# Later tokens' scores in one stretch over four banks, and norm sums as two split products with ones

## The chip, the core and the metric

The kernel runs on one core of a Trainium2 chip, in one launch. A core has TensorE (matrix products from SBUF into the eight banks of PSUM; PE in the trace, PEld its weight loads), VectorE (DVE), ScalarE (ACT) and GpSimd (POOL), each with a queue of its own that it works off in order, and SyncE (SP), which here issues the transfers from and to memory. The metric is device time in microseconds of one execution; less is better.

## The reference, cut to what matters

Two layers work on 256 tokens of a prompt and 32 later tokens of another request, 288 columns in all, with a model width of 1024. A layer is

```
x += 0.5 * swiglu1(rmsnorm(x))                      # 1024 -> 2816 -> 1024
z  = rmsnorm(x) @ w_in                              # 1024 -> 2560: q, k, v | pool | conv
x += concat(diffattn(q, k, v), pool(u), conv(...)) @ w_out
x += 0.5 * swiglu2(rmsnorm(x))
rmsnorm(x) = x / sqrt(mean(x*x) + 1e-6) * gain
```

The attention has 4 heads, each with two halves of 64 channels. Each half has scores and a softmax of its own, and the head's weights are `softmax(half 0) - lam * softmax(half 1)`. A later token attends to 512 cached keys and to the 32 new ones. The final norm follows the second layer. Everything is float32, and the result has to agree to nearly that accuracy.

## The kernel before, in words

Tokens lie along the free dimension: x is eight tiles of [128 channels, 288 tokens]. A weight product in full precision is made of three products in the format float32r, which runs at the ordinary pace of the array: a number is split into a high part and a remainder, and `mm3` (L247) issues high x high, remainder x high and high x remainder. Weights arrive in chunks of 1 MB; ScalarE copies a chunk to its high part `wh` (L108; in the mixer through L477), and VectorE subtracts to get the remainder `wl` (L109; L477). The same is done to x (`xh`, `xl`) behind each residual. Plain float32 products are left where both operands are activations: scores, turnings, weighted sums, the pooling's small product, and sums over channels by a product with ones.

The norm is put off: the products run on x times gain, and the result is multiplied by R, one over the root of the mean square of a token. The sum of squares over the eight tiles is one tile `ssum` [128, 288]; its sum over the 128 partitions comes from TensorE. There are three ways. `stats_a` and `stats_last` (first and last norm, not changed) and the mixer's `stats` (L514) take three products of one column with `ssum` as weights, so that tokens lie on partitions, raise to the power -0.5 on GpSimd, put the three columns on diagonals, and spread them by a float32 product of ones with the diagonals (L528); sinR and cosR read that product's bank, then ScalarE copies it to R. `stats_wide` (L228, the three later FFNs) multiplies ones by `ssum` in float32 (L231), so that each partition has the sums, and VectorE gets 1/sqrt by a bit trick and three Newton steps.

TensorE's instructions run in the order of the code. In `ffn` the code of `stats_wide` stands after the fifth of eight k tiles of the first pair of products (L319), and the other engines' instructions are ordered by the tile framework: by the age of an instruction in the code, among those that are ready. In `mixer` the order of ScalarE, VectorE and GpSimd is written out by hand too, by a planner. All work beside the projections is a task in stages. A clock counts 0.369 us per triple of products, costs of the other engines are added up per queue (`charge`), and a stage is issued once its operands should stand by that clock (`poll`). A stage that needs a PSUM buffer asks for it with `wait("sc")` (one buffer of two banks, for scores) or `wait("tp")` (two buffers of one bank, for all that is turned or summed); each request adds LAG 0.2 and MARGIN 1.1 us to its time.

`attn_s` (L664) is the later tokens' attention. For each half it asks for the score buffer, makes the scores of the four heads over 544 keys in two blocks of 272, head h in output partitions 32h to 32h+31 (L673), takes the maximum over both blocks, and makes the exponentials with their sum. The halves follow each other through the one buffer. Then come the combination, five turnings, the product with the values (L708) and `finish`, which splits the result into operands of the output projection. That projection takes its input tiles in the order 4, 5, 0, 1, 2, 3, 6, 7, two at a time; the later tokens' result is asked for with tile 0 (L864). Before the mixer's products a dummy activation loads ScalarE's table for exponentials (L832), behind the first half of the output projection one loads the table for SiLU (L871).

Of the kernel before, what the change touches and what calls it, by code (L numbers as in the profile page):

```python
# [9 lines left out]
F32 = mybir.dt.float32  # L10
# [8 lines left out]
P = 128  # L19
# [37 lines left out]
def tile_step(ctx, tc, xT, w_gu, w_dn, w_in, w_out, par, con, lamv, ck, cvp, pw,  # L57
# [66 lines left out]
    ones = const.tile([P, P], F32, tag="ones", name="ones")  # L124
    V.memset(ones, 1.0)
    act0 = const.tile([P, 1], F32, tag="act0", name="act0")
# [17 lines left out]
    def warm_up(n):  # L144
        """keeps the tensor engine's clock up while it has to wait"""
        warm = ps_a.tile([P, 512], F32, tag="acc", name="warm")
        for _ in range(n):
            PE.matmul(warm[:, 0:P], ones, ones, start=True, stop=True)
# [3 lines left out]
    make_identity(nc, ident)  # L152
    mhalf = const.tile([P, 3], F32, tag="mhalf", name="mhalf")
    G.memset(mhalf, -0.5)

# [5 lines left out]
    def operands(k, g):  # L161
        """x tile k is final for this phase: operands of the next products"""
# [6 lines left out]
    def square(k, apart=0):  # L169
        """sum of squares"""  # L170
# [17 lines left out]
    def stats_a():  # L188
        """1/rms per token, tokens on partitions, then on the diagonals of [128, T]"""
# [7 lines left out]
    def stats_last(part, pss):  # L197
        """the same at the end: the sum over the tiles before the last one goes ahead"""
# [28 lines left out]

    def stats_wide():  # L228
        """1/rms per token on all partitions at once: bit trick and three Newton steps"""
        ps = ps_t.tile([P, 512], F32, tag="tp", name="ps_w")  # L230
        PE.matmul(ps[:, :T], ones, ssum[0], start=True, stop=True)  # L231
# [25 lines left out]
    # lambda of each layer, the gains of the head norm  # L257
# [91 lines left out]
    def mixer(l, g_next):  # L349
        with tc.tile_pool(name="mp", bufs=1) as mp, tc.tile_pool(name="mt", bufs=2) as mt, \  # L350
# [18 lines left out]
            # Everything beside the projections' products is a task in stages. A stage is issued once its  # L369
            # operands should stand, by a clock of the products issued so far and of the other engines'  # L370
            # queues, so that no queue is held up for long by what it waits for.
# [82 lines left out]
            def wait(res=None, cost=0.0, dep=None):  # L454
                return (0.0, res, cost, dep)
# [58 lines left out]
            def stats():  # L514
                ps = ps_t.tile([P, 512], F32, tag="tp", name="ps_ss")
                for b, (t0, _, _) in enumerate(TB):
                    PE.matmul(ps[:, b:b + 1], ssum[0][:, t0:t0 + P], ones[:, 0:1], start=True, stop=True)
                a = tmp.tile([P, 3], F32, tag="rs_a", name="rs_a")
                V.tensor_scalar(a, ps[:, 0:3], 1.0 / D, EPS, ALU.mult, ALU.add)
                r = tmp.tile([P, 3], F32, tag="rs_r", name="rs_r")  # L520
                G.tensor_tensor(r, a, mhalf, ALU.pow)
                yield wait()
                dg = tmp.tile([P, T], F32, tag="rs_d", name="rs_d", bufs=1)
                for b, (_, o, n) in enumerate(TB):
                    V.tensor_scalar(dg[:, b * P:b * P + n], ident[:, o:o + n], r[:, b:b + 1], None, ALU.mult)
                yield wait()
                ps = ps_t.tile([P, 512], F32, tag="tp", name="ps_r")
                PE.matmul(ps[:, :T], ones, dg, start=True, stop=True)  # L528
                V.tensor_tensor(sinR, con_t[:, K_SIN:K_SIN + T], ps[:, :T], ALU.mult)
                V.tensor_tensor(cosR, con_t[:, K_COS:K_COS + T], ps[:, :T], ALU.mult)  # L530
                yield wait()
                R[0] = tmp.tile([P, T], F32, tag="R", name="R")
                S.activation(R[0], ps[:, :T], AF.Copy)
# [97 lines left out]
            def finish(o, s1, n, dst, key):  # L631
                """o: PSUM [q, n blocks of e]; normalise over e, turn, scale, split into the mix operands"""
# [31 lines left out]
            def attn_s():  # L664
                yield wait(dep=("q", 3))
                yield wait(dep=("k", 3))
                for c in range(2):
                    yield wait("sc", 1.0)
                    sc = ps_s.tile([P, 2, 512], F32, tag="sc", name="scs")
                    r = slice(64 * c, 64 * c + 64)  # L670
                    for b in range(2):
                        for h in range(H):
                            PE.matmul(sc[32 * h:32 * h + 32, b, 0:272], qT[h][r, SEQ:T],  # L673
                                      kts[r, h, b * 272:(b + 1) * 272], start=True, stop=True)
                    yield wait()
                    nm = mt.tile([P, 1], F32, tag="nms", name="nms")
                    V.tensor_reduce(nm, sc[:, :, 0:272], AX.XY, ALU.max)
                    V.tensor_scalar(nm, nm, -0.125, None, ALU.mult)
                    yield wait()
                    S.activation(es_t[:, c, :].rearrange("p (b k) -> p b k", b=2), sc[:, :, 0:272], AF.Exp,  # L680
                                 scale=0.125, bias=nm, accum_out=sms[:, c:c + 1])
                    release("sc")
                yield wait()
                fr = mt.tile([P, 1], F32, tag="frs", name="frs")
# [320 lines left out]
```

## Time and profile before

| what | value |
|---|---|
| median of 3 runs | 1085.14 us (1084.9, 1085.14, 1089.98) |
| profiled execution, span from first to last instruction | 1083.4 us (the page gives no other time of this execution) |
| TensorE busy | 1070.1 us (99%), 8100 matmuls |
| VectorE busy | 702.3 us (65%) |
| ScalarE busy | 529.7 us (49%) |
| GpSimd busy | 50.0 us (5%) |
| granted TensorE clock, mean | 0.997 |

The stages, in us from the start of the span: first norm and start to 25.9, first FFN to 223.6, mixer to 331.8, second FFN to 542.4; layer 1 the same way: to 752.9, 861.2, 1072.0; then the last norm. TensorE's busy time overlaps from one matmul to the next, and the ends of matmuls are modelled; so a product's cost is read from the starts of the matmuls around it. A float32 call shows as two instructions, x2.

### The profile page before, as it was taken

What the parts mean: (1) busy time and instruction counts of PE and PEld (TensorE: products, weight loads), DVE (VectorE), ACT (ScalarE), POOL (GpSimd) and SP (SyncE); (2) the same over time, 40 slices, a digit from 0 to 9 for tenths busy, and PEclk for the clock granted to TensorE, in tenths of its full rate; (3) what the DMA queues carried; (4) which work ended last, traced back from release to release, by engine and by line L of the source; (5) the groups of instructions that cost most, each with busy time, mean ns of one, the idle gap of its engine ahead of it and who ended that gap; (6) DMA issues with size and microseconds to landing.
All of it is one profiled execution on the core that took longest, in us unless ns stands there. A gap on an engine that the chain in (4) does not pass through costs nothing.

```text
span 1083.4 us, 19614 instructions
## 1 busy us (share of the span) xinstructions
PE 1070.1 (99%) x8100; PEld 1058.2 (98%) x8100; DVE 702.3 (65%) x1191; ACT 529.7 (49%) x920; POOL 50.0 (5%) x78
## 2 busy tenths in 40 slices
PE   8999999999999999999999999999999999999997
PEld 7999999999999999999999999999999999999997
DVE  7766664547878766654576666554779786666442
ACT  6444444448755444444444444443785644444431
POOL 6000000011200000000000000000112000000000
PEclk9999999999999999999999999999999999999999
DMA  7544444445445444444444444444444354444421
GB/s 277 200 175 156 160 185 162 156 166 170 139 157 194 177 174 155 160 172 175 156 156 174 178 155 160 173 173 164 169 140 155 124 230 171 180 156 158 174 97 44
DMA packets 33897, 178.66 MB, mean 165 GB/s; under 512 B 7808, under 2 KB 10624, under 8 KB 13328
## 3 DMA queue, kind: packets, MB, share of 16 engines
q1 hardware_dynamic: 33456, 176.90, 45.5%
q8 instruction: 63, 1.03, 0.4%
q10 hardware_dynamic: 288, 0.44, 0.1%
q14 instruction: 26, 0.21, 0.1%
q0 software_dynamic: 64, 0.07, 0.0%
HBM read 173.80 MB, written 3.61 MB: 164 GB/s over the span
## 4 chain that ended last, share of the span: by engine, by line
PE 70%; issue 23%; ACT 3%; DVE 2%; DMA 1%; SPq 0%; POOLq 0%; POOL 0%; DVEq 0%; ACTq 0%
PE acc L250 22%; PE acc L251 22%; PE acc L252 22%; ACT zw L477 2%; ACT e L477 1%; ACT wh L477 1%; PE sc L250 1%; PE sc L251 1%; DMA xall<-in_xT 1%; PE sc L252 1%; DVE wl L477 0%; PE scs L673 0%; PE sc L587 0%; DVE wl L109 0%; DVE yg L899 0%
## 5 line engine op out<-in xcount | busy, mean ns | idle before, releaser
L250 PE MATMUL acc<-xh,wh 128*128 128x288 f32 x1664 | 495.9, 298 | 0.0
L251 PE MATMUL acc<-xh,wl 128*128 128x288 f32 x1664 | 493.0, 296 | 1.3 <-DVE wl L477 0.6
L252 PE MATMUL acc<-xl,wh 128*128 128x288 f32 x1664 | 491.1, 295 | 2.7 <-DVE xl L167 2.7
L109 DVE TENSOR_TENSOR wl<-raw,wh 128x1024 fp32r<-128x1024 f32 (+2 forms) x272 | 328.5, 1210 | 189.8 <-ACT wh L108 189.6
L108 ACT ACTIVATE wh<-raw 128x1024 fp32r<-128x1024 f32 (+2 forms) x272 | 280.4, 1034 | 301.8 <-PE acc L252 261.9
L252 PEld LDWEIGHTS acc<-xl,wh 128*128 128x128 f32 x1664 | 314.8, 189 | 3.6 <-DVE xl L167 3.6
L250 PEld LDWEIGHTS acc<-xh,wh 128*128 128x128 f32 x1664 | 314.7, 189 | 2.3 <-issue 1.3
L251 PEld LDWEIGHTS acc<-xh,wl 128*128 128x128 f32 x1664 | 313.0, 188 | 3.5 <-DVE wl L477 1.8
L250 PE MATMUL acc<-hh,wh 128*128 128x288 f32 x704 | 208.4, 296 | 0.0
L251 PE MATMUL acc<-hh,wl 128*128 128x288 f32 x704 | 207.7, 295 | 0.0
L252 PE MATMUL acc<-hl,wh 128*128 128x288 f32 x704 | 207.0, 294 | 0.0
L252 PEld LDWEIGHTS acc<-hl,wh 128*128 128x128 f32 x704 | 132.6, 188 | 0.0
L251 PEld LDWEIGHTS acc<-hh,wl 128*128 128x128 f32 x704 | 132.2, 188 | 0.0
L250 PEld LDWEIGHTS acc<-hh,wh 128*128 128x128 f32 x704 | 131.9, 187 | 0.0
L297 ACT ACTIVATE hh<-t 128x288 fp32r<-128x288 f32 x88 | 38.9, 444 | 107.9 <-DVE t L296 107.9
L477 DVE TENSOR_TENSOR wl<-raw,wh 128x512 fp32r<-128x512 f32 x112 | 76.6, 700 | 5.9 <-ACT wh L477 5.8
L477 ACT ACTIVATE wh<-raw 128x512 fp32r<-128x512 f32 x112 | 65.6, 627 | 6.6 <-PE acc L252 4.1
L298 DVE TENSOR_TENSOR hl<-t,hh 128x288 fp32r<-128x288 f32 x88 | 40.1, 457 | 40.0 <-ACT hh L297 39.8
L291 DVE TENSOR_TENSOR t<-acc,R 128x288 f32<-128x288 f32 x84 | 38.3, 456 | 32.4 <-PE acc L252 32.3
L294 ACT ACTIVATE t<-t 128x288 f32<-128x288 f32 x88 | 37.5, 426 | 7.6 <-DVE t L291 7.6
L296 DVE TENSOR_TENSOR t<-t,t 128x288 f32<-128x288 f32 x88 | 39.5, 450 | 0.0
L342 DVE SCALAR_TENSOR_TENSOR xall<-acc,xall 128x288 f32<-128x288 f32 x32 | 14.6, 456 | 37.0 <-PE acc L252 36.8
(181 smaller groups left out, 773.6 us busy)
## 6 DMA issues: line engine op xcount, KB each, us to landing
raw<-in_w_gu SPq DMA_DIRECT2D x86, 1024.0 KB, 4.8
raw<-in_w_dn SPq DMA_DIRECT2D x44, 1024.0 KB, 4.8
raw<-in_w_in SPq DMA_DIRECT2D x20, 1024.0 KB, 4.8
raw<-in_w_out SPq DMA_DIRECT2D x8, 1024.0 KB, 5.0
kts<-in_ck SPq DMA_DIRECT2D x2, 1024.0 KB, 5.4
cvt<-in_cv SPq DMA_DIRECT2D x2, 1024.0 KB, 7.2
raw<-in_w_gu SPq DMA_DIRECT2D x2, 512.0 KB, 7.4
out<-k SPq DMA_DIRECT2D x8, 128.0 KB, 1.7
```

What stands on the lines that cost most here:

```text
L108: S.activation(wh[:, sl, :], src, AF.Copy)
L109: V.tensor_tensor(wl[:, sl, :], src, wh[:, sl, :].bitcast(F32), ALU.subtract)
L250: PE.matmul(acc, wh[:, b, :], mh, start=first, stop=False)
L251: PE.matmul(acc, wl[:, b, :], mh, start=False, stop=False)
L252: PE.matmul(acc, wh[:, b, :], ml, start=False, stop=last)
L291: V.tensor_tensor(t1, ag[:, :T], R, ALU.mult)
L294: S.activation(t1, t1, AF.Silu)
L296: V.tensor_tensor(h, t1, t2, ALU.mult)
L297: S.activation(hh[j], h, AF.Copy)
L298: V.tensor_tensor(hl[j], h, hh[j].bitcast(F32), ALU.subtract)
L342: V.scalar_tensor_tensor(xs[m], acc[:, :T], 0.5, xs[m], ALU.mult, ALU.add)
L477: return f(out, *a, **kw)
```

## The change

Later tokens' scores: `attn_s` asks for the score buffer and for both "tp" buffers, and then makes all scores in one stretch: first 32 columns (the new keys) of each head and half into the two "tp" banks, then 512 columns (the cached keys) into the two banks of the score buffer, half c in a bank of its own. The 32 columns are copied to SBUF and the "tp" buffers given back, four small reductions and a maximum give the two halves' maxima, and the exponentials are made in four pieces whose sums are added.

Norm sums: `spread_split` splits `ssum` into a float32r high part (ScalarE) and a remainder (VectorE), and `spread_sum` multiplies both by ones in float32r. `stats_wide` takes its sums from there, and the mixer's `stats` too, which then has the sums on all partitions: ScalarE takes the root, VectorE the reciprocal and one Newton step, and sinR, cosR and R come from SBUF. The dummy activation ahead of the mixer now loads the table for the root, and one behind the root loads that for exponentials. Comments that were taken out are left out here.

```
+    ones_r = const.tile([P, P], F32R, tag="ones_r", name="ones_r")
...
+    V.tensor_copy(ones_r, ones)
...
+    eps_t = const.tile([P, 1], F32, tag="eps", name="eps")
+    G.memset(eps_t, EPS)
...
+    def spread_split(S, V):
+        sh = tmp.tile([P, T], F32R, tag="rs_u", name="rs_h", bufs=1)
+        sl = tmp.tile([P, T], F32R, tag="rs_y", name="rs_l", bufs=1)
+        S.activation(sh, ssum[0], AF.Copy)
+        V.tensor_tensor(sl, ssum[0], sh.bitcast(F32), ALU.subtract)
+        return [sh, sl]
+    def spread_sum(parts):
+        ps = ps_t.tile([P, 512], F32, tag="tp", name="ps_w")
+        for n in range(2):
+            PE.matmul(ps[:, :T], ones_r, parts[n], start=n == 0, stop=n == 1)
+        parts.clear()
+        return ps
     def stats_wide():
-        ps = ps_t.tile([P, 512], F32, tag="tp", name="ps_w")
-        PE.matmul(ps[:, :T], ones, ssum[0], start=True, stop=True)
+        ps = spread_sum(spread_split(S, V))
...
             def stats():
-                ps = ps_t.tile([P, 512], F32, tag="tp", name="ps_ss")
-                for b, (t0, _, _) in enumerate(TB):
-                    PE.matmul(ps[:, b:b + 1], ssum[0][:, t0:t0 + P], ones[:, 0:1], start=True, stop=True)
-                a = tmp.tile([P, 3], F32, tag="rs_a", name="rs_a")
-                V.tensor_scalar(a, ps[:, 0:3], 1.0 / D, EPS, ALU.mult, ALU.add)
-                r = tmp.tile([P, 3], F32, tag="rs_r", name="rs_r")
-                G.tensor_tensor(r, a, mhalf, ALU.pow)
-                yield wait()
-                dg = tmp.tile([P, T], F32, tag="rs_d", name="rs_d", bufs=1)
-                for b, (_, o, n) in enumerate(TB):
-                    V.tensor_scalar(dg[:, b * P:b * P + n], ident[:, o:o + n], r[:, b:b + 1], None, ALU.mult)
-                yield wait()
-                ps = ps_t.tile([P, 512], F32, tag="tp", name="ps_r")
-                PE.matmul(ps[:, :T], ones, dg, start=True, stop=True)
-                V.tensor_tensor(sinR, con_t[:, K_SIN:K_SIN + T], ps[:, :T], ALU.mult)
-                V.tensor_tensor(cosR, con_t[:, K_COS:K_COS + T], ps[:, :T], ALU.mult)
-                yield wait()
-                R[0] = tmp.tile([P, T], F32, tag="R", name="R")
-                S.activation(R[0], ps[:, :T], AF.Copy)
+                parts = spread_split(S, V)
+                yield wait()
+                ps = spread_sum(parts)
+                r = tmp.tile([P, T], F32, tag="R", name="R")
+                a = tmp.tile([P, T], F32, tag="rs_d", name="rs_w", bufs=1)
+                u = tmp.tile([P, T], F32, tag="rs_y", name="rs_t", bufs=1)
+                S.activation(r, ps[:, :T], AF.Sqrt, scale=1.0 / D, bias=eps_t)
+                nc.scalar.activation(act0, r[:, 0:1], AF.Exp, scale=0.0)
+                charge("act", 1.4)
+                V.tensor_scalar(a, ps[:, :T], 1.0 / D, EPS, ALU.mult, ALU.add)
+                yield wait()
+                V.reciprocal(r, r)
+                V.tensor_tensor(u, r, r, ALU.mult)
+                V.scalar_tensor_tensor(u, u, -0.5, a, ALU.mult, ALU.mult)
+                V.scalar_tensor_tensor(r, u, 1.5, r, ALU.add, ALU.mult)
+                R[0] = r
+                yield wait()
+                V.tensor_tensor(sinR, con_t[:, K_SIN:K_SIN + T], r, ALU.mult)
+                V.tensor_tensor(cosR, con_t[:, K_COS:K_COS + T], r, ALU.mult)
...
             def attn_s():
                 yield wait(dep=("q", 3))
                 yield wait(dep=("k", 3))
+                yield wait("sc")
+                yield wait("tp")
+                yield wait("tp", 1.3)
+                tn = [ps_t.tile([P, 512], F32, tag="tp", name="scn") for _ in range(2)]
+                sc = ps_s.tile([P, 2, 512], F32, tag="sc", name="scs")
+                for dst, k0, n in ((tn, PAST, DEC), ([sc[:, 0, :], sc[:, 1, :]], 0, PAST)):
+                    for h in range(H):
+                        for c in range(2):
+                            r = slice(64 * c, 64 * c + 64)
+                            PE.matmul(dst[c][32 * h:32 * h + 32, 0:n], qT[h][r, SEQ:T], kts[r, h, k0:k0 + n],
+                                      start=True, stop=True)
+                yield wait()
+                sn = mt.tile([P, 2, DEC], F32, tag="sn", name="sn", bufs=1)
                 for c in range(2):
-                    yield wait("sc", 1.0)
-                    sc = ps_s.tile([P, 2, 512], F32, tag="sc", name="scs")
-                    r = slice(64 * c, 64 * c + 64)
-                    for b in range(2):
-                        for h in range(H):
-                            PE.matmul(sc[32 * h:32 * h + 32, b, 0:272], qT[h][r, SEQ:T],
-                                      kts[r, h, b * 272:(b + 1) * 272], start=True, stop=True)
-                    yield wait()
-                    nm = mt.tile([P, 1], F32, tag="nms", name="nms")
-                    V.tensor_reduce(nm, sc[:, :, 0:272], AX.XY, ALU.max)
-                    V.tensor_scalar(nm, nm, -0.125, None, ALU.mult)
-                    yield wait()
-                    S.activation(es_t[:, c, :].rearrange("p (b k) -> p b k", b=2), sc[:, :, 0:272], AF.Exp,
-                                 scale=0.125, bias=nm, accum_out=sms[:, c:c + 1])
-                    release("sc")
-                yield wait()
+                    S.activation(sn[:, c, :], tn[c][:, 0:DEC], AF.Copy)
+                    release("tp")
+                nm = mt.tile([P, 4], F32, tag="nms", name="nms")
+                V.tensor_reduce(nm[:, 0:2], sc, AX.X, ALU.max)
+                V.tensor_reduce(nm[:, 2:4], sn, AX.X, ALU.max)
+                V.tensor_tensor(nm[:, 0:2], nm[:, 0:2], nm[:, 2:4], ALU.max)
+                V.tensor_scalar(nm[:, 0:2], nm[:, 0:2], -0.125, None, ALU.mult)
+                yield wait()
+                for c in range(2):
+                    S.activation(es_t[:, c, 0:PAST], sc[:, c, :], AF.Exp, scale=0.125, bias=nm[:, c:c + 1],
+                                 accum_out=sms[:, c:c + 1])
+                release("sc")
+                for c in range(2):
+                    S.activation(es_t[:, c, PAST:], sn[:, c, :], AF.Exp, scale=0.125, bias=nm[:, c:c + 1],
+                                 accum_out=sms[:, 2 + c:3 + c])
+                yield wait()
+                V.tensor_tensor(sms[:, 0:2], sms[:, 0:2], sms[:, 2:4], ALU.add)
...
-            nc.scalar.activation(act0, xl[0][:, 0:1].bitcast(F32), AF.Exp, scale=0.0)
+            nc.scalar.activation(act0, xl[0][:, 0:1].bitcast(F32), AF.Sqrt, scale=0.0)
```

## Rows read from the trace of the kernel before

**Rows 1.** Windows: us; busy us and instructions of PE, PEld, DVE, ACT, POOL; clock; DMA.
```profile
153.30:223.60 70.30, 70.30 (x530) 70.30 (x528) 35.74 (x46) 31.29 (x42) 0.00 (x0) 1.00 0.45 165
223.60:306.30 82.70, 81.58 (x658) 77.09 (x657) 62.69 (x163) 56.44 (x159) 15.23 (x26) 1.00 0.46 156
```

**Rows 2.** Waits of PE over the span: us in total, times, longest.
```profile
PE sc L587 <- ACT e L477: 1.4, 2, 0.7
...
PE acc L251 <- DVE wl L477: 0.6, 2, 0.3
```

**Rows 3.** Timeline (start, duration, instruction): first score stretch of later tokens.
```profile
281.70 0.29 PE L252 MATMUL acc<-xl,wh 128*128 128x288 f32 x1
...
283.22 0.29 PE L251 MATMUL acc<-xh,wl 128*128 128x288 f32 x1
```

**Rows 4.** Instructions of tile scs: count, shortest/median/longest ns.
```profile
L673 PE MATMUL scs<-kts,q x64: 389/389/413, 281.9 to 816.8; 64*32 64x272 f32 x64
L477 DVE TENSOR_REDUCE nms<-scs x4: 712/714/717, 283.9 to 818.5; 128x1 f32<-128x544 f32 x4
```

**Rows 5.** Timeline: norm sum of layer 0's second FFN.
```profile
335.95 0.65 PE L231 MATMUL ps_w<-sq,ones 128*128 128x288 f32 x2
...
336.56 0.29 PE L251 MATMUL acc<-xh,wl 128*128 128x288 f32 x1
```

**Rows 6.** Timeline, PE: scores of the first tokens, head 3.
```profile
276.81 0.29 PE L252 MATMUL acc<-xl,wh 128*128 128x288 f32 x1
277.04 0.71 PE L587 MATMUL sc<-k,q 64*128 64x256 f32 x4
277.57 0.39 PE L588 MATMUL sc<-k,q 64*128 64x128 f32 x4
...
278.14 0.29 PE L251 MATMUL acc<-xh,wl 128*128 128x288 f32 x1
```

**Rows 7.** Timeline: the mixer's norm products, layer 0.
```profile
227.73 0.72 PE L517 MATMUL ps_ss<-ones,sq 128*128 128x1 f32 x6
...
228.53 0.29 PE L251 MATMUL acc<-xh,wl 128*128 128x288 f32 x1
...
230.78 0.65 PE L528 MATMUL ps_r<-rs_d,ones 128*128 128x288 f32 x2
...
231.40 0.29 PE L251 MATMUL acc<-xh,wl 128*128 128x288 f32 x1
```

**Rows 8.** Timeline: later tokens' result, and the output projection's first product.
```profile
306.17 0.35 DVE L477 SCALAR_TENSOR_TENSOR ml<-tpo,gsub,mh 128x128 fp32r<-128x128 f32 x1
...
306.36 0.29 PE L250 MATMUL acc<-mh,wh 128*128 128x288 f32 x1
```

**Rows 9.** Timeline: the norm's end in the mixer, layer 0.
```profile
231.47 0.45 DVE L477 TENSOR_TENSOR sinR<-con,ps_r 128x288 f32<-128x288 f32 x1 [0.61 <-PE ps_r L528]
...
232.32 0.41 ACT L477 ACTIVATE R<-ps_r 128x288 f32<-128x288 f32 x1 [7.02 <-DVE cosR L477]
```

**Rows 10.** Groups by line and form, ACT: busy us, mean ns | idle before.
```profile
L832 ACT ACT_TABLE_LOAD x2 | 2.6, 1283 | 0.0
```

**Rows 11.** Timeline, DVE: around the norm sum of layer 0's second FFN.
```profile
334.69 0.45 DVE L477 TENSOR_TENSOR sq<-sq 128x288 f32<-128x288 f32 x1
...
335.66 1.22 DVE L109 TENSOR_TENSOR wl<-raw,wh 128x1024 fp32r<-128x1024 f32 x1
336.80 0.45 DVE L233 TENSOR_SCALAR rs_w<-ps_w 128x288 f32<-128x288 f32 x1
```

**Rows 12.** Timeline, DVE, ACT and PE: the same place of layer 1's first FFN.
```profile
545.40 0.45 DVE L176 TENSOR_TENSOR sq<-sq 128x288 f32<-128x288 f32 x1
...
545.94 1.06 ACT L108 ACTIVATE wh<-raw 128x1024 fp32r<-128x1024 f32 x1 [1.39 <-PE acc L252]
...
546.48 0.65 PE L231 MATMUL ps_w<-sq,ones 128*128 128x288 f32 x2
...
547.04 1.23 DVE L109 TENSOR_TENSOR wl<-raw,wh 128x1024 fp32r<-128x1024 f32 x1 [1.19 <-ACT wh L108]
```

## The prediction, on record before the changed kernel ran

> **What bounds the kernel now.** I read the windows by stage first. In a stretch of plain products TensorE is busy for the whole of it: 530 matmuls in 70.30 us, 0.133 us each, at full granted clock, while VectorE and ScalarE work about half of the time [rows 1]. The mixer's first 82.7 us hold the small work as well: TensorE is busy for 81.58, VectorE for 62.69, ScalarE for 56.44. So the sum of what TensorE issues sets the time, and a change pays only by what it takes out of TensorE's queue or by a wait that it removes there. The waits come second: outside the start TensorE waits for the scores' buffer (1.4 us in all) and for split weights (0.6 us), both in the mixers, and hardly anywhere else [rows 2]. Third the timeline, for what each small product costs TensorE beyond the pace of 0.133.
>
> **Scores of the later tokens.** Now: a stretch of 8 calls x 272 columns (16 instructions, as each float32 call is issued in two parts). The last ordinary matmul before it starts at 281.70, so the next was due at 281.83; the second one behind it starts at 283.22, so the first was due to start at 283.09. The stretch costs 1.25 us [rows 3]. There are 64 such instructions, hence four stretches, 5.0 us [rows 4].
>
> What float32 columns cost comes from the norm sum: 288 columns push the matmuls behind them from 335.95 to 336.56 less one pace, 0.48 us, or 1.66 ns a column [rows 5]. 8 x 272 columns one after the other would be 3.6 us. In 1.25 us they can only have run four heads at a time, each in its own 32 output partitions: 544 columns, 0.90 us, and 0.35 us of edges. That the two halves (operand partitions 0 to 63 and 64 to 127, two banks) overlap too is seen at the first tokens' scores: 768 columns in four calls would be 1.27 us in a row, yet they take 278.14 - 0.133 - 276.94 = 1.06 us with edges [rows 6], so 0.35 us of edges leave 0.7, about half of 1.27.
>
> After: per layer one stretch. Each of the eight places (four heads x two halves) gets 32 + 512 columns, 544, again 0.90 us if all eight run together. Edges 0.35. The 16 instructions of 32 columns: nothing below, and above 0.11 us each if they run singly, as the six one-column instructions of the old norm sum do (0.67 us / 6) [rows 7], 1.8 us. The nearest row is the present stretch, whose 16 instructions show no cost beyond columns and edges, so I take 0.15. That is 1.4 us against 2.5: 1.1 us saved a layer, **2.2 us** in all. Ends: 1.25 us saved a layer with no extra; 0.5 us lost (0.90 + 0.35 + 1.8 against 2.5).
>
> Around it: the stage now asks for the score buffer and both "tp" buffers, and the planner adds 0.2 + 1.1 us to each request, so it starts 2.6 us after the old first stretch, or behind the turning of head 3 if that takes a buffer first, near the old second one. One reduction over 1024 columns in place of 544 (0.71 us) [rows 4] adds 0.6 us, and the exponentials, now in four pieces behind it, I take at 0.9 more. The result was ready at 306.52, its first use is due 8 triples of 0.4 us after 306.36, at 309.6 [rows 8]: the 3 us of slack hide it. Without that cover 1.5 us a layer would show. Holding both "tp" buffers keeps head 3's and the pooling's small products back, which are due only behind the same point.
>
> **Norm sums in the mixers.** Removed: three one-column products, from 227.73 until 228.53 less a pace, 0.67 us, and the product that spreads the result, from 230.78 until 231.40 less a pace, 0.49 us [rows 7]. Added: two products of 288 columns in the ordinary format, two paces, 0.27 us. Saved 0.89 us a layer, **1.8 us**. Their operands need one ScalarE copy and one VectorE subtraction after the sum of squares; ScalarE stands idle for 7 us there, until 232.32 [rows 9], so they stand two microseconds before TensorE comes to them. GpSimd's power step and the diagonal go. ScalarE gets a root and a second table load (1.28 us) [rows 10]: with the two products some three triples behind 227.7, at 228.9, 0.3 for them, 0.45 for the root, 1.28 and 0.2 for the load and its dummy, it is free at 231.1, and the rotary copies that now follow the copy of R at 232.73 can start earlier. VectorE gets a reciprocal and three passes more (about 0.45 us each by the 288-column sinR row [rows 9], some 2 us), so sinR and cosR come up to 1.5 us later. Net effect on the 2.0 us of waits in the mixers: zero taken, ends -1.4 and +1.5 us a layer. No row shows a wide reciprocal; at several times a plain pass the upper end would apply.
>
> **Norm sums of the three later FFNs.** The product: 0.48 becomes 0.27, 0.21 us each, 0.6 us in all. But the place in TensorE's queue stays (after the fifth triple pair), and the copy and the subtraction are now ahead of it. In layer 0's second FFN the sum of squares starts its last addition at 334.69 for 0.45 us, done 335.14; TensorE comes at 335.95 [rows 5, 11]. The slack is 0.8 us, and ScalarE (0.41, as the copy of R) [rows 9] plus VectorE (0.45) plus hand-overs need about 1.0 if both queues are free. VectorE's isn't: at 335.66 it takes a weight remainder of 1.22 us, which was written before the norm in the code and so goes first, and only then, at 336.80, the norm's own step. The subtraction would take that place: 336.80 to 337.25, TensorE resumes about 337.3. Stall 1.35 us, and all that is queued behind on TensorE is the next FFN's products. Lower end 0.25 us (subtraction first), upper end 2.6 us (two remainders first). The same order holds in layer 1. In layer 1's first FFN the addition ends at 545.85, VectorE is then free until 547.04, and ScalarE takes a weight piece at 545.94; TensorE was due at 546.48 [rows 12]. If the copy goes ahead of that piece (it is older in the code), the stall is 0.45 us; behind it, 2.2. I take 0.45. Stalls: 2 x 1.35 + 0.45 = **3.2 us**, ends 1.0 and 7.4.
>
> **Sum.** -2.2 - 1.8 - 0.6 + 3.2 = -1.4 us on the profiled span of 1083.4, so 1082.0. The median of the runs, 1085.14, lies 1.74 us above that span (the page gives no time of its own for the profiled run); 1082.0 + 1.7 = **1083.7 us**.
>
> The Trainium skill, "TensorE: Matmul & The Clock Gate", Part 3, states that matmuls start and end strictly in program order. The code writes 256 and 128 columns of one half and then of the other, and the trace has all four 256-column instructions ahead of the four 128-column ones [rows 6]: what reaches the engine is not the code's order, so the halves of one call need not follow each other. If the new stretch did reach it as written, that rule gives the first rival below.
>
> **Rivals.**
> (1) The halves don't pair with the heads: only neighbouring calls overlap, the two halves of a head, and the heads follow each other: 4 x 0.90 + 0.35 = 3.95 us a layer against 2.5. It speaks for it that the new loop has the halves innermost; against it that [rows 6] show instructions regrouped across calls. Then +2.9 in place of -2.2: 1088.8 us, slower than before; it decides once a stretch takes over 2.1 us, where the total passes 1085.1.
> (2) The FFN stalls stay small, because the copy and the subtraction are put ahead of the weight work: 3 x 0.3 in place of 3.2 gives 1081.4; with ScalarE's earlier start taking half of the 2.0 us and their restarts, 1079.5. VectorE free in [rows 12] speaks for it, [rows 11] against.
> (3) The mixer's head turns worse: the longer VectorE chain delays the rotated heads, TensorE waits 1.5 us more a layer: 1086.7. Against it: ScalarE, the engine that those waits name, starts earlier.
>
> **Chances.** Forecast 0.55 (its own range 1082.0 to 1085.5), (1) 0.10, (2) 0.22, (3) 0.13. The range from 1079.2 to 1088.0 leaves out most of (1) and the tail of (2). A measurement can tell about 0.5%, 5.4 us. Faster than 1079.7 needs (2) in full: 0.11. Slower than 1090.6 needs (1) with the upper stalls, or (3) with them: 0.06. The rest, 0.83, is no change.
>
> **What would show it.** Score stretches of 1.4 us, one a layer, instructions starting eight at a time (right), or 4 us (rival 1). Two ordinary products for each norm sum, no one-column products. A wait of TensorE on the norm's subtraction at each later FFN, 1.35 us behind a weight remainder in both second FFNs; if these rows are missing, rival 2. Waits for the scores' buffer and split weights in the mixers near 2.0 us; well over that is rival 3. The prediction is wrong in its reasons if the stalls and the savings don't appear in these places, even where the total fits.

## The result, and the profile after

The changed kernel takes 1092.6 us (median of 5 runs, 1092.37 to 1097.42) against 1085.15 us of the kernel before on the same chip: ratio 1.0069, 95% interval 1.0052 to 1.0087. The change makes the kernel slower by 0.7%; the prediction was 1083.7 us, a little faster. The profiled span went from 1083.4 to 1090.7 us.

To see where the 7.3 us arose, I cut both traces at the first weight product of each stage. "Mixer" runs from the first input product to the first output product; "FFN" is the first half of one of the three later FFNs, which holds its norm. A "pace" below is the 0.133 us from one ordinary product to the next [rows 1], and a "split weight" is a remainder `wl` that VectorE makes for the products.

| stage, us | before | after | difference |
|---|---|---|---|
| first norm and first FFN's first half | 148.00 | 148.40 | +0.40 |
| mixer, layer 0 and 1 | 82.63, 82.67 | 84.74, 85.15 | +2.11, +2.48 |
| FFN, in order | 140.15, 140.15, 140.15 | 141.25, 140.29, 141.24 | +1.10, +0.14, +1.09 |
| all other stages | 344.3 | 344.3 | 0.0 |

Three windows of the trace after (the mixer of layer 0 and the two halves of the FFN behind it) say the same; columns as in [rows 1]. The mixer is longer although TensorE's busy time in it fell from 81.58 to 81.24 us: TensorE waits. The second half of the FFN, plain products only, is as before, and the granted clock is 1.00 in all three windows.

```profile
224.10:308.90 84.80, 81.24 (x652) 75.72 (x651) 66.45 (x165) 59.77 (x170) 14.47 (x25) 1.00 0.45 143
334.50:475.70 141.20, 140.14 (x1059) 139.91 (x1059) 98.67 (x150) 64.67 (x91) 0.00 (x0) 1.00 0.48 173
475.70:546.10 70.40, 70.40 (x530) 70.40 (x529) 36.88 (x46) 29.63 (x38) 0.00 (x0) 1.00 0.45 165
```

TensorE's waits after (us in total, times, longest), where [rows 2] had 1.4 us for the scores' buffer and 0.6 us for split weights:

```profile
PE acc L270 <- DVE wl L496: 4.6, 9, 0.9
...
PE ps_w L244 <- DVE rs_l L237: 2.1, 2, 1.1
PE yp L780 <- DVE pd L496: 1.4, 2, 0.7
...
PE sc L606 <- ACT e L496: 1.0, 2, 0.7
```

The wait for split weights in the mixers grew from 0.6 to 4.6 us, and two groups are new: the norm's remainder in the FFNs (2.1) and a pooling product (1.4). The wait for the scores' buffer did not grow (1.0). Split weights and scores' buffer together are 5.6 us, where the prediction had named about 2.0 for its forecast and "well over that" as the sign of its rival 3.

**The score stretch**, timeline of TensorE in layer 0, the counterpart of [rows 3]. All 16 instructions of 32 columns start between 287.80 and 287.90. Those of 512 columns start eight at a time, the first eight between 287.88 and 287.93, the second eight between 288.32 and 288.36, so all eight places (four heads, two halves) run together.

```profile
287.57 0.30 PE L271 MATMUL acc<-xl,wh 128*128 128x288 f32 x1
287.80 0.27 PE L695 MATMUL scn<-kts,q 64*32 64x32 f32 x13
...
287.90 1.05 PE L695 MATMUL scs<-kts,q 64*32 64x512 f32 x13
288.88 0.40 PE L269 MATMUL acc<-xh,wh 128*128 128x288 f32 x1
289.12 0.29 PE L270 MATMUL acc<-xh,wl 128*128 128x288 f32 x1
```

Read as in the prediction: from 287.57 plus a pace to 289.12 less a pace is 1.29 us, where 1.4 was predicted and two stretches of 1.25 stood before. The mixer's norm products are the two ordinary ones foreseen:

```profile
229.32 0.29 PE L244 MATMUL ps_w<-rs_h,ones_r 128*128 128x288 f32 x1
229.45 0.30 PE L244 MATMUL ps_w<-rs_l,ones_r 128*128 128x288 f32 x1
229.59 0.29 PE L269 MATMUL acc<-xh,wh 128*128 128x288 f32 x1
```

**The FFN's norm**, layer 0's second FFN, all engines, the counterpart of [rows 11]. VectorE takes a weight remainder of 1.22 us at 338.17, and the norm's remainder stands behind it. The second product was due a pace behind the first, at 338.59, and starts at 339.81:

```profile
338.17 1.22 DVE L109 TENSOR_TENSOR wl<-raw,wh 128x1024 fp32r<-128x1024 f32 x1
...
338.46 0.29 PE L244 MATMUL ps_w<-rs_h,ones_r 128*128 128x288 f32 x1
339.31 0.45 DVE L237 TENSOR_TENSOR rs_l<-sq,rs_h 128x288 fp32r<-128x288 f32 x1
...
339.81 0.40 PE L244 MATMUL ps_w<-rs_l,ones_r 128*128 128x288 f32 x1 [1.06 <-DVE rs_l L237]
```

**The mixer's head**, VectorE in layer 0, the counterpart of [rows 9]. The brackets at the end of a line give the idle time before it and who ended it.

```profile
230.32 0.46 DVE L496 TENSOR_SCALAR rs_w<-ps_w 128x288 f32<-128x288 f32 x1 [3.07 <-ACT R L496]
230.69 0.68 DVE L496 TENSOR_TENSOR wl<-raw,wh 128x512 fp32r<-128x512 f32 x1
231.83 1.95 DVE L496 RECIPROCAL R<-R 128x288 f32<-128x288 f32 x1 [0.46 <-ACT act L541]
233.89 0.46 DVE L496 TENSOR_TENSOR rs_t<-R 128x288 f32<-128x288 f32 x1
234.39 0.46 DVE L496 SCALAR_TENSOR_TENSOR rs_t<-rs_t,rs_w 128x288 f32<-128x288 f32 x1
234.88 0.46 DVE L496 SCALAR_TENSOR_TENSOR R<-rs_t,R 128x288 f32<-128x288 f32 x1
235.25 0.68 DVE L496 TENSOR_TENSOR wl<-raw,wh 128x512 fp32r<-128x512 f32 x1
235.85 0.45 DVE L496 TENSOR_TENSOR sinR<-con,R 128x288 f32<-128x288 f32 x1
236.22 0.45 DVE L496 TENSOR_TENSOR cosR<-con,R 128x288 f32<-128x288 f32 x1
```

cosR is done at 236.67; before, the copy that cosR released started at 232.32 [rows 9]. The start was 0.4 us longer, and beyond that cosR comes 4.0 us later, where the prediction had up to 1.5. The reciprocal alone takes 1.95 us, and VectorE stands idle for 0.46 us before it, until ScalarE's dummy activation is done. ScalarE's side:

```profile
229.79 0.50 ACT L496 ACTIVATE R<-ps_w,eps 128x288 f32<-128x288 f32 x1 [2.50 <-PE ps_w L244]
230.31 1.28 ACT L541 ACT_TABLE_LOAD   x1
231.60 0.20 ACT L541 ACTIVATE act<-R 128x1 f32<-128x1 f32 x1
```

The root is ready at 230.29. The dummy reads R, the reciprocal writes over R, so the reciprocal may start only when the dummy is through, at 231.80. The split weights that TensorE needs queue behind all this: TensorE's first long stop is behind the product at 237.56.

```profile
237.56 0.29 PE L269 MATMUL acc<-xh,wh 128*128 128x288 f32 x1
238.70 0.40 PE L270 MATMUL acc<-xh,wl 128*128 128x288 f32 x1 [0.85 <-DVE wl L496]
```

The split that ends this stop was slow itself: it took 1.10 us, where one with nothing beside it takes 0.68. GpSimd was at two products with sinR, which the late sinR had let pile up:

```profile
236.48 1.62 POOL L496 TENSOR_TENSOR zw<-zw,sinR 128x288 f32<-128x288 f32 x2 [209.73 <-ACT wh L496]
...
237.54 1.10 DVE L496 TENSOR_TENSOR wl<-raw,wh 128x512 fp32r<-128x512 f32 x1
```

**The pooling product.** Near the mixer's end TensorE stops once more, at 301.24, for 0.87 us beyond a pace:

```profile
301.24 0.29 PE L271 MATMUL acc<-xl,wh 128*128 128x288 f32 x1
302.25 0.72 PE L780 MATMUL yp<-pd,pw_t 128*128 128x288 f32 x2 [0.71 <-DVE pd L496]
```

### The profile page after: what moved, and what is told of

Its sections match the earlier page's. It is cut to its first block, busy times and chain, and to the rows that moved or that the text cites. A ratio compares the mean times of both kernels' runs of the same rounds, so it can differ in the third digit from the quotient of the medians.

```text
span 1090.7 us, 19621 instructions
## 1 busy us (share of the span) xinstructions
PE 1069.2 (98%) x8088; PEld 1055.2 (97%) x8088; DVE 711.2 (65%) x1201; ACT 536.1 (49%) x941; POOL 50.8 (5%) x77
## 4 chain that ended last, share of the span: by engine, by line
PE 64%; issue 23%; DVE 6%; ACT 4%; POOL 2%; DMA 0%; SPq 0%; POOLq 0%; DVEq 0%; ACTq 0%
PE acc L269 20%; PE acc L270 20%; PE acc L271 20%; DVE wl L496 2%; ACT zw L496 1%; ACT e L496 1%; POOL sq L184 1%; POOL sq L188 1%; PE sc L270 1%; PE sc L269 1%; PE sc L271 1%; ACT wh L496 1%; DMA xall<-in_xT 0%; DVE nm L496 0%; DVE R L496 0%
## 5 line engine op out<-in xcount | busy, mean ns | idle before, releaser
L496 DVE TENSOR_TENSOR wl<-raw,wh 128x512 fp32r<-128x512 f32 x112 | 79.1, 725 | 4.2 <-ACT wh L496 3.8
L496 POOL TENSOR_TENSOR zw<-zw,sinR 128x288 f32<-128x288 f32 x16 | 12.9, 811 | 719.5 <-ACT wh L496 671.8
```

The lines of the kernel that those rows point to most:

```text
L496: return f(out, *a, **kw)
```

## The experiments

Theory A: the mixers lose their time at the head, where VectorE's chain became longer, above all by a 1.95 us reciprocal that the prediction had put at 0.45 and the planner at 0.07 + 288/960 = 0.37 us. Rivals: the score stretch, which needs three buffers at once, holds the mixer up (B); ScalarE's table loads do (C); the further passes do (D).

All stages cut as above, from each kernel's own profile; ratios to the kernel before run on the same chip, with 95% interval ("one run": a single execution, so no ratio). The kernel before took 1086.1 to 1086.3 us (median) beside the experiments, 1 us more than the 1085.15 that the expectations start from. A mixer that a kernel leaves untouched takes 82.51 to 82.67 us, so differences of 0.16 us and less say nothing.

| kernel | ratio | mixers | FFNs |
|---|---|---|---|
| before | 1 | 82.63, 82.67 | 140.15, 140.15, 140.15 |
| changed | 1.0069 (1.0052 to 1.0087) | 84.74, 85.15 | 141.25, 140.29, 141.24 |
| scores only | 1.0011 (0.9999 to 1.0023) | 82.69, 82.75 | 140.14, 140.14, 140.14 |
| FFN norm only | 1.0022 (1.0009 to 1.0034) | 82.55, 82.51 | 141.25, 140.32, 141.25 |
| mixer norm only | 1.0065 (1.0049 to 1.0081) | 84.52, 84.93 | 140.15, 140.15, 140.15 |
| changed, no reciprocal | 1.0041 (1.0024 to 1.0058) | 83.17, 83.51 | 141.25, 140.32, 141.25 |
| changed, dummy's operand | one run | 84.25, 84.68 | 141.25, 140.32, 141.25 |
| changed, logarithm and exponential | 1.0014 (1.0004 to 1.0023) | 82.27, 82.60 | 141.25, 140.32, 141.29 |
| scores, pooling later | 0.9998 (0.9988 to 1.0008) | 82.49, 82.49 | 140.15, 140.15, 140.15 |
| scores, pooling and turning later | 0.9978 (0.9966 to 0.9991) | 81.78, 81.82 | 140.15, 140.15, 140.15 |
| FFN norm, product later | one run | 82.55, 82.55 | 139.92, 139.92, 139.92 |
| all mended, old mixer norm | 0.9971 (0.9960 to 0.9983) | 81.77, 81.73 | 139.92, 139.92, 139.92 |
| all mended | 0.9958 (0.9943 to 0.9974) | 81.33, 81.24 | 139.92, 139.92, 139.92 |
| two constants only | 0.9996 (0.9986 to 1.0007) | 82.51, 82.53 | 140.15, 140.14, 140.15 |

**The scores alone.** `stats_wide` and the mixer's `stats` as before, `attn_s` as changed.

> The kernel before with only the later tokens' scores of the changed kernel; the norm sums are the old ones. Theory A (the mixer's extra time comes from its new head chain, with the 1.95 us reciprocals on VectorE): the two score stretches become one of 1.3 us, -1.1 us a layer, so 1082.8 us, and the pooling product's extra wait of 0.7 us a layer doesn't come. Theory A2 (that wait belongs to the scores' wider work on VectorE and ScalarE): 1084.5 us. Rival B (one stretch that holds both transposition banks is what costs the mixer): slower than before, 1087 us or more.

Nothing gained: +0.06 and +0.08 us in the mixers in place of -1.1 each. The pooling wait is there with the old norm too, as theory A2 said, though A2 still had 0.65 us left to gain. The prediction's saving falls, and so does rival B as the cause of the mixers' 4.6 us. Timeline of TensorE in this kernel:

```profile
299.62 0.29 PE L272 MATMUL acc<-xl,wh 128*128 128x288 f32 x1
300.63 0.72 PE L781 MATMUL yp<-pd,pw_t 128*128 128x288 f32 x2 [0.71 <-DVE pd L497]
301.28 1.08 PE L742 MATMUL os<-cvt,aTs 128*32 128x128 f32 x32
```

In the kernel before, the later tokens' products of attention and values came first (298.68) and the pooling product behind them (301.77); now the planner has put the pooling product in front, while VectorE is not done with its operand. The stop costs 0.87 us of the 1.2 us that the score stretches save. Most of the rest goes at the two turnings of the exponentials, which cost 0.17 and 0.15 us more than before by the starts of the products around them; why they do stays open.

**The FFN's norm alone.** `attn_s` and the mixer's `stats` as before.

> The kernel before with only the FFN's norm sum split into two products (scores and mixer as before). All theories: VectorE's subtraction of 0.45 us and the copy ahead of it move the norm product back behind squares and operands, TensorE waits 1.35, 0.4 and 1.35 us at the three places instead of nothing, less 0.2 us saved in each product: 1085.15 + 2.3 = 1087.5 us. If the stage differences seen in the changed kernel came from elsewhere (the mixer's lateness handed on): 1085 us.

+2.4 us by the ratio, +2.37 by the three stages (1.10, 0.17, 1.10), as expected and as in the changed kernel.

**The mixer's norm alone.** `attn_s` and `stats_wide` as before.

> The kernel before with only the mixers' new norm chain (split sum, wide root, reciprocal and Newton step). Theory A: TensorE waits for tiles that VectorE frees late, some 4 us a layer, less 0.9 us saved in the norm products: 1090 to 1092 us. Rival B (the scores' stretch costs the mixer): 1084 to 1086 us. Rival C (the table of the root loaded on ScalarE, then that of the exponentials, is what is late): 1090 to 1092 us as in A, and the run without reciprocals tells A from C.

Ratio and stages put the loss here and not in the scores: +1.89 and +2.26 us in the mixers, 4.15 in all, with the norm's 0.89 us a layer of saved products already in it. The timed 7.1 us (5.3 to 8.8) are more than that. The profile is of the fastest of the five runs, and its start was 1.8 us longer than before; what the rest is stays open.

**No reciprocal.**
```
-                V.reciprocal(r, r)
+                V.tensor_scalar(r, r, 1.0, None, ALU.mult)
```


> The changed kernel with the 128x288 reciprocal of the mixers' norm replaced by a multiplication by 1.0 of the same shape and place (so the norm's value isn't computed); the same instructions otherwise. Theory A: the pass goes from 1.95 to about 0.45 us, the chain on VectorE ends 1.5 us earlier in each mixer, and TensorE's waits for VectorE's tiles shrink by more than that since the plan's charge is right again: 1092.6 less 3 to 6 us, 1086.6 to 1089.6 us. Rival C (ScalarE's table loads hold the chain): within 1 us of the changed kernel, 1091.6 to 1092.6 us. Rival D (the chain's four further VectorE passes, not the reciprocal's length): 1091 to 1092 us.

This kernel leaves the reciprocal out and keeps its place and its charge in the plan. The mixers fall by 1.57 and 1.64 us, the pass by 1.64 (1.95 to 0.31). So what the reciprocal costs at the end is about its length, and C and D don't carry that part. Not all of it need be the pass itself: the first split weight behind the head is shorter too, 0.75 us in both layers against 1.10 and 1.18. Theory A had asked for more than that, since the plan's charge of 0.37 us is about true here: 3 to 6 us in all, and 3.2 were found. VectorE's timeline of this run:

```profile
231.30 0.68 DVE L496 TENSOR_TENSOR wl<-raw,wh 128x512 fp32r<-128x512 f32 x1
232.44 0.31 DVE L496 TENSOR_SCALAR R<-R 128x288 f32<-128x288 f32 x1 [0.46 <-ACT act L541]
232.85 0.46 DVE L496 TENSOR_TENSOR rs_t<-R 128x288 f32<-128x288 f32 x1
```

The 0.46 us in front of it are still there; this much of the loss is rival C's.

**The dummy's operand.**
```
-                nc.scalar.activation(act0, r[:, 0:1], AF.Exp, scale=0.0)
+                nc.scalar.activation(act0, ones[:, 0:1], AF.Exp, scale=0.0)
```


> The changed kernel with one operand changed: the dummy exponential that fetches the table reads the constant ones instead of the root's tile, which the reciprocal overwrites. Theory: the reciprocal no longer waits for the table load of 1.28 us and the dummy of 0.2 us; it starts behind VectorE's split at 231.4 instead of 231.83, 0.45 us earlier, and each mixer gains 0.3 to 0.5 us: 1092 us. Rival (that wait is hidden by the split): no change, 84.7 and 85.1 us.

-0.49 and -0.47 us in the mixers, the length of that wait. The one time, 1093.16 us, is not below the changed kernel's; its start took 150.02 us, 1.6 more. The reciprocal follows the split weight at once:

```profile
232.31 0.68 DVE L496 TENSOR_TENSOR wl<-raw,wh 128x512 fp32r<-128x512 f32 x1
232.91 1.95 DVE L496 RECIPROCAL R<-R 128x288 f32<-128x288 f32 x1
```

**Logarithm and exponential.** R is first exp(-0.5 ln(mean square)), then the Newton step as before.
```
-                S.activation(r, ps[:, :T], AF.Sqrt, scale=1.0 / D, bias=eps_t)
-                nc.scalar.activation(act0, r[:, 0:1], AF.Exp, scale=0.0)
-                charge("act", 1.4)
+                S.activation(u, ps[:, :T], AF.Ln, scale=1.0 / D, bias=eps_t)
+                S.activation(r, u, AF.Exp, scale=-0.5)
...
-                V.reciprocal(r, r)
...
-            nc.scalar.activation(act0, xl[0][:, 0:1].bitcast(F32), AF.Sqrt, scale=0.0)
+            nc.scalar.activation(act0, ones[:, 0:1], AF.Ln)
```


> The changed kernel with the mixers' root, reciprocal and table change replaced by a logarithm and an exponential on ScalarE, 0.4 to 0.5 us each, followed by the same Newton step; all of the computation is there. Theory A (the reciprocal's 1.95 us, and its start behind the table's dummy): VectorE's chain starts 0.5 us after the norm product instead of 2.0 us and lacks the 1.95 us, so each mixer falls from 84.9 to about 83 us, 1092.6 - 4 = 1088.6 us, or 83.3 if a table load of 1.28 us is put between the two. Rival (the four longer VectorE passes behind it are what counts): each mixer stays above 84 us.

-2.47 and -2.55 us a mixer, a little more than A said: 1.0014 in place of 1.0069. The rival, that the longer passes behind are what counts, falls. ScalarE's timeline shows a table load between the two functions, and the chain is shorter all the same:

```profile
230.35 0.50 ACT L496 ACTIVATE rs_t<-ps_w,eps 128x288 f32<-128x288 f32 x1 [1.21 <-PE ps_w L244]
230.87 1.28 ACT L496 ACT_TABLE_LOAD   x1
232.16 0.44 ACT L496 ACTIVATE R<-rs_t 128x288 f32<-128x288 f32 x1
```

From the start of the activation that reads the norm sum to a first R it takes 2.25 us (230.35 to 232.60); in the changed kernel 4.0 (229.79 to 233.78).

**Pooling product later** (scores alone otherwise). The first number is a delay in the plan; g is the pooling group, 0 or 1.
```
-                yield wait("tp", 0.48)
+                yield (1.5 * g, "tp", 0.48, None)
```


> The kernel before with the new scores alone, and the second pooling group's product made due 1.5 us later in the plan, which puts it behind the later tokens' 20 products of attention and values instead of ahead of them. Theory (the scores' own 1.1 us a layer is real and was given back because TensorE stood 1.0 us in front of that pooling product): the wait goes, each mixer takes 81.6 us instead of 82.7, 1085.1 - 2.1 = 1083.0 us on the scale of the kernel before. Rival (VectorE and ScalarE are simply full there, the order doesn't matter): another product waits in its place, each mixer stays at 82.7 us and the time at 1085 us.

0.20 and 0.26 us of 1.1 came through. As the rival said, another product waits in the place of the first, the turning of the later tokens' result:

```profile
305.72 0.29 PE L272 MATMUL acc<-xl,wh 128*128 128x288 f32 x1
306.48 0.33 PE L672 MATMUL tpo<-ident,on 128*128 128x128 f32 x1 [0.46 <-ACT on L497]
```

**Both later.** As above, and in `finish`:
```
-                yield wait("tp", 0.22 * n)
+                yield (1.0 if key == "ms" else 0.0, "tp", 0.22 * n, None)
```


> The kernel before with the new scores alone, the second pooling group's product due 1.5 us later and the transposition of the later tokens' result due 1.0 us later in the plan. Theory (the time that the scores save is handed back at whichever product on TensorE comes in front of its late operand; the result itself isn't needed until 3 us into the output projection): the wait of 0.75 us in front of the transposition goes too, each mixer takes 81.7 us against 82.65 before, 1085.1 - 1.9 = 1083.2 us. Rival (VectorE and ScalarE are full, the lateness goes on to the output projection): 82.3 to 82.5 us a mixer, 1084.6 us.

As the theory said: 81.78 and 81.82, -0.85 us a layer, ratio 0.9978. Of this 0.08 a layer has only moved behind the cut: the turning now stands at the first output product, and the output projection takes 25.67 us in place of 25.59. So 0.77 us a layer is gained. VectorE and ScalarE were not full; TensorE had only stood in front of operands that were not ready.

**FFN product later.** The FFN's norm alone, its product after the eighth k tile in place of the fifth.
```
-                    if not first and (j, k) == (0, 4):
+                    if not first and (j, k) == (0, 7):
```


> The kernel before with only the FFN's norm sum split, and its product issued three k-steps of the first output tile later (1.2 us). Theory (TensorE waits only because the copy and the subtraction of 0.45 us stand behind the squares and operands on their engines): the waits of 1.1, 0.2 and 1.1 us go, and each FFN's first stage takes 140.0 us, 0.15 less than before, 1084.7 us. Rival (the product's result is late for whatever comes next, so the wait moves to the first tile's scaling): 140.6 to 141.2 us.

The stage takes 139.92 us at all three places, 0.23 less than before, about the 0.21 us that the cheaper product saves; the rival, that the wait moves on, falls. TensorE is busy for the whole of it (the window of layer 0's second FFN):

```profile
336.96:476.88 139.92, 139.92 (x1060) 139.92 (x1059) 98.41 (x150) 64.56 (x91) 0.00 (x0) 1.00 0.50 175
```

Its one time, 1089.38 us, holds a start of 153.1 us, in which TensorE waited 4.8 us for GpSimd's squares.

**All mended together**, with the new mixer norm (logarithm and exponential) and with the old one:

> The changed kernel with its three faults taken away together: logarithm and exponential instead of root and reciprocal in the mixers, the FFN's norm product three k-steps later, the pooling product and the later tokens' transposition due later. Theory: each mixer 81.3 to 81.6 us, each FFN's first stage 139.9 us, 1085.1 - 2.3 - 0.7 = 1082.1 us, under the kernel before. Rival (the parts get into each other's way on VectorE): 1084 to 1086 us.

> As the one before, but with the mixers' norm as in the kernel before (three narrow products, POOL's power, diagonals). Theory: each mixer 81.7 us, each FFN's first stage 139.9 us, 1085.1 - 1.9 - 0.7 = 1082.5 us. The difference to the one before is what the new norm of the mixers is worth once it has no reciprocal: 0.2 to 0.8 us; by the rival (a longer VectorE chain can't be worth it) this one is the faster of the two.

1082.7 against 1086.23 us of the kernel before on the same chip (0.9958, 0.9943 to 0.9974): with these repairs the change is a gain of 0.4%. With the old mixer norm it is 1083.67 us. By the stages the new norm is worth 0.44 and 0.49 us a mixer once the reciprocal is gone; the two ratios' intervals overlap, so the times alone don't show it.

**Two constants.** The first five kernels with the new constants show starts of 148.4 to 149.8 us, against 148.0 before, which raised the question whether the constants delay it.

> The kernel before with only two constants more in its start (a copy of the 128x128 ones on VectorE, a 128x1 fill on POOL). The first FFN's first stage, before the first mixer, took 148.0 us in the one profile of before and 148.4 to 150.0 in most profiles of the kernels with these constants. Theory (this is how the first loads happen to land, not the constants): 1085.1 us, ratio within 0.1% of 1. Rival (the constants delay the first operands): 0.5 to 1.5 us slower, 1085.6 to 1086.6 us.

The times show no delay: 0.9996, and the interval's upper end of 0.8 us leaves only the lower part of the rival's 0.5 to 1.5; this profile's start is 148.48 us. Kernels that issue the same work in the start differ in TensorE's waits there, for the first operands and for GpSimd's squares (1.1 us in the changed kernel, 4.8 in the one above).

## Why the prediction was wrong

By its own terms, on the span (1082.0 predicted, 1090.7 found, 8.7 us apart):

- **The mixer's norm is the step that failed most.** "Net effect on the 2.0 us of waits in the mixers: zero taken, ends -1.4 and +1.5 us a layer." The products saved what was said (0.27 us in place of 1.16), but the mixers with this part alone are 1.89 and 2.26 us longer, so the head costs 2.8 and 3.15 us a layer, beyond the upper end. In all 4.15 us in place of -1.8, 5.95 of the 8.7. The term that failed is "sinR and cosR come up to 1.5 us later": it was 4.0. The reciprocal in it was taken at 0.45 us "by the 288-column sinR row", though no row showed one; it is 1.95, and 1.6 us a layer of the loss goes when it goes. Another 0.48 is a dependence that the diff showed and the text overlooked: the dummy reads the tile that the reciprocal overwrites. The remaining 0.7 to 1.0 us a layer fits the three Newton passes of 0.46 with the split weight between them; it was not tested by itself. A plan that charges the reciprocal its true length wasn't tried either.
- **The upper end wasn't carried through.** The text said that "at several times a plain pass the upper end would apply", yet that case was given no time of its own, and rival 3, which names this mechanism, was priced at 1.5 us a layer (1086.7 us) and argued away by ScalarE's earlier start; a time above 1090.6 got a chance of 0.06. ScalarE did start its copies earlier (232.35 against 232.74), and it didn't matter: the chain ran through VectorE.
- **Scores: the stretch was right (1.29 for 1.4), the cover was not.** The stretch came near the old second one and the result itself was hidden, both as said. But "keeps head 3's and the pooling's small products back, which are due only behind the same point" failed: the plan brought the pooling product in front of its operand, and TensorE stood there for 0.87 us. -2.2 predicted, +0.14 found, 2.3 of the 8.7. The kernel with both products later shows that 0.77 us a layer, not 1.1, were to be had.
- **FFN: right, in the place and in the cause.** Stalls less the saved product 2.6 us, found 2.33: the second product starts 1.35 us behind the first in both second FFNs, behind a weight remainder as foreseen, and 0.39 in layer 1's first. Rival 2 falls, as does rival 1: all eight places ran together.
- The FFNs came out 0.3 below the forecast. The rest is the start, 0.4, and 0.3 that the parts cost more together than one by one.

**Why layer 1 loses more than layer 0.** The traces show a part of the remainder that the prediction had no term for. Where a split weight starts behind one of GpSimd's products with sinR, it takes what is left of that product and about 0.55 us more, where it takes 0.68 alone (last section). In layer 1's mixer TensorE waits on such a split (lines below): it took 1.25 us, against 0.90 before and 0.89 in the kernel with all mended. All profiled kernels that make this split in 1.24 to 1.25 us have a layer 1 that is 0.33 to 0.43 us longer than layer 0; in those with 0.89 to 0.91 the two differ by 0.09 at most. That is a reading of the traces; no run moved this split alone.

```profile
793.40 0.81 POOL L496 TENSOR_TENSOR zw<-zw,sinR 128x288 f32<-128x288 f32 x1
...
793.51 1.25 DVE L496 TENSOR_TENSOR wl<-raw,wh 128x512 fp32r<-128x512 f32 x1 [0.20 <-ACT wh L496]
...
794.82 0.40 PE L270 MATMUL acc<-xh,wl 128*128 128x288 f32 x1 [0.68 <-DVE wl L496]
```

The Trainium skill, "ScalarE: Activation LUTs", section "What it computes", advises VectorE's reciprocal and ScalarE's root for a reciprocal root, the pair that the change uses in the other order; the section names no price for it. Here the pair took 4.0 us to a first R, with the wait for the dummy in it, and the logarithm with the exponential 2.25, a table load included, with the same Newton step behind either; ScalarE's own reciprocal root, of which the page warns, was not run.

## What to carry to other kernels

An operation that the trace doesn't show at its width needs an upper bound of several plain passes, and this bound belongs in a rival with its own time, above all when it enters the one engine on which the others' operands queue. Time saved in TensorE's queue is worth only what the next product with a late operand doesn't take back: look for the next such product, and move it behind others that are ready. When a tile gets a second reader only to fetch a table, see who overwrites that tile.

## What the runs showed of the hardware

At 288 columns a reciprocal on VectorE took four times as long as a product of two tiles. By line and form in the changed kernel (count, busy us, mean ns, idle before):

```profile
L496 DVE RECIPROCAL R<-R 128x288 f32<-128x288 f32 x2 | 3.9, 1954 | 0.9 <-ACT act L541 0.9
...
L496 DVE RECIPROCAL fr<-sm 128x2 f32<-128x2 f32 x8 | 1.3, 164 | 2.9 <-ACT e L496 2.8
```

An estimate from these two widths is (1954 - 164) / 286 = 6.3 ns a column. The product of two tiles of 288 columns takes 450 to 460 ns. The narrow reciprocals, which stood in the kernel before too (162 ns), give no hint of it.

A table load on ScalarE took 1283 ns each time, and the neighbours stood close: in the changed kernel the load starts 0.02 us after the root ends and the dummy 0.01 us after the load.

A split weight on VectorE (two inputs, 512 columns) that starts while GpSimd is at a product with sinR took what was left of that product plus about 0.55 us. In the changed kernel 0.55 us were left at 237.54 and the split took 1.10; 0.70 were left at 793.51 and it took 1.25. With nothing on GpSimd it takes 0.68 us. Beside GpSimd's small power step on two columns it stayed at 0.68.
